# A hybrid recurrent decoder layer on one core: output projection in one pair of PSUM banks, layer norm transposes after the next block's gates and GLU, one Newton root for two tiles, gates ahead of GLU

## The chip, the cores and the metric

The kernel runs on one core of a Trainium2 chip. The metric is the device time of one execution in microseconds (us). The engines are called as in the profile: PE (matrix engine), PEld (its weight loads), DVE (vector), ACT (activation), POOL (GpSimd), SP (sync, which issues DMAs).

## What is computed

One decoder layer over 2048 prompt rows and 32 sample rows of width 1024, all in float32:

```python
z = h @ in_proj                                   # [gate | xa | xb], 512 columns each
xa_c = causal_dwconv(xa)                          # width 4
r, gi = sigmoid(xa_c @ w_r + b_r), sigmoid(xa_c @ w_i + b_i)
a = exp(-8 * r * softplus(-lam))
hseq = linear_scan(a, sqrt(1 - a * a) * gi * xa_c)
y_a = gelu(gate) * hseq
gy = gelu(s5_ssm(xb))
y_b = gy * sigmoid(gy @ glu_w + glu_b)            # the GLU
mix = concat([y_a, y_b]) @ out_proj
x = layer_norm(ALPHA * x + g1 * mix)
f = square(relu(h2 @ mlp_w1 + b1)) @ mlp_w2       # h2: x, scaled and shifted
x = layer_norm(ALPHA * x + g2 * f)
```

Float32 products are made of three matmuls on split operands (high x high, low x high, high x low), so that each operand is split beforehand into a high part (a copy on ACT) and a low part (a subtraction on DVE or POOL).

## The kernel before, in words

The program has four stages: modulation, input projection and the S5 scan (to about 440 us of the trace), then the stage that the change touches (about 440 to 765 us), then the MLP in three groups of rows (to the end). The stage in the middle goes over the prompt in eight blocks `pi` of 256 rows, each with these pieces:

- `rg_gates` (L301): eight gate products of 3 matmuls, 256 columns wide, each into a bank of its own; ACT takes each out with a Sigmoid, then makes four Tanh tiles `th` from the results. 24 matmuls a block.
- `glu_block` (L896): loads `gy` (four DMAs on SP, L850), splits it, makes four GLU tiles of 12 matmuls (48 a block), a Tanh in place on the bank (ACT, L913), and takes each out with `stt` into `gy` on DVE (L914); then splits the product into `ybh` and `ybl`.
- `out_block` (L930): two tiles of 128 rows, each with two halves of 512 columns. One half is 24 matmuls of 512 columns into one bank (L962 to L964); DVE multiplies the bank by the gate row (L965) and adds the row of x, scaled (L966), after which the bank is free. So four such outputs and 96 matmuls a block. The x rows come by one DMA a tile on SP (L935) into `raw`, a pool of three buffers.
- `norm` (L976), after each tile: statistics of the two halves (L981), their aggregate, the inverse root of the variance by an integer first guess and three Newton rounds on 128x1 columns (`rstd_of`, L626: ten DVE instructions a tile), the scaled row (L984), eight PE transposes into the two banks `C` (L995), two ACT copies into `nT` (L996; one buffer, tag `res`) and one DMA to `Nd` on SP (L997). The MLP reads `Nd`.
- `rg_scan` (L321): Exp, Square, DVE product, Sqrt on ACT (the "root" in the table order), two POOL products, four DVE scans (L347), the product `gt` and its split `yah`, `yal`.
- `rg_conv` (L271): the convolution on DVE, and its split.

The loop over `pi` (L1019) writes them in the order GLU of block `pi+1`, gates of `pi+2`, output of `pi`, scan of `pi+2`, convolution of `pi+3`. This order is not the order of the queues: the framework takes it as the priority of each instruction and fixes each engine's queue when the program is built, by a model of the times. On the chip each queue is then strictly in order. `after_all` adds order alone, here between ACT functions that need different tables: GLU Tanh after the Sqrt of the block's scan, Exp after the block's Sigmoids and after an earlier GLU's Tanh.

PSUM has eight banks under four tags `A` to `D`, two each. Gates and GLU take `A` and `B` in turn, the outputs `D` and `B` in turn (L204), the transposes `C`. The MLP's first products use `A`, `D`, `B`. In the last block (`pi == 7`) the 32 sample rows come first (`oq`, L946), the first MLP weights and operands are made beside it (`first_h`, L687), and the norms of the two prompt tiles are put off into the MLP (`deferred`).

Of the kernel before, what the change touches and what calls it, by code (L numbers as in the profile page):

```python
# [13 lines left out]
ALU = mybir.AluOpType  # L14
# [21 lines left out]
def trunk(ctx: ExitStack, tc: tile.TileContext, *args):  # L36
# [167 lines left out]
    GLU_BANKS, OUT_BANKS = "AB", "DB"  # L204
# [421 lines left out]
    def rstd_of(pool, mv, nm, np_):  # L626
        r = pool.tile([P, 1], F32, tag="rstd", name=nm, bufs=2)[:np_]
        v = pool.tile([P, 1], F32, tag="rvar", name=nm + "v", bufs=2)[:np_]
        t = pool.tile([P, 1], F32, tag="rtmp", name=nm + "t", bufs=2)[:np_]
        ts(V, v, mv[:, 1:2], EPS, None, ALU.add)  # L630
        V.tensor_scalar(t.bitcast(I32), v.bitcast(I32), 1, None, ALU.arith_shift_right)
        V.tensor_scalar(r.bitcast(I32), t.bitcast(I32), -1.0, 1597463007.0, ALU.mult, ALU.add)
        ts(V, v, v, -0.5, None, ALU.mult)
        for _ in range(3):
            stt(t, r, v, r, ALU.mult, ALU.mult)
            stt(r, t, 1.5, r, ALU.add, ALU.mult)
        return r
# [258 lines left out]
    def glu_block(pi):  # L896
# [27 lines left out]
        if pi:  # L924
            after_all(rgs[pi]["root"], glu_t)
        if pi < 7:
            rgs["glu", pi + 1] = glu_t
        return yh, yl

    def out_block(pi, ya, yb):  # L930
        t0 = pi * 256
        tiles = ([(256, TS, True)] if pi == 7 else []) + [(0, P, False), (P, P, False)]
        for ti, (o, w, smp) in enumerate(tiles):
# [33 lines left out]
            work = lambda *x, at=(pi, ti, xt, w, smp, t0 + o): norm(*at, *x)  # L967
            if pi == 7 and ti in DEFER:
                deferred.append(work)
            else:  # L970
                work(p4)
# [4 lines left out]
    def norm(pi, ti, xt, w, smp, t, pool):  # L976

        st = pool.tile([P, 2, 6], F32, tag="st5", name=f"st_{pi}_{ti}", bufs=2)
        mv = pool.tile([P, 2], F32, tag="mv5", name=f"mv_{pi}_{ti}", bufs=2)
        for half in range(2):  # L980
            V.bn_stats(st[:w, half, :], xt[:w, half * 512:half * 512 + 512])  # L981
        V.bn_aggr(mv[:w], st[:w])
        rs = rstd_of(pool, mv[:w], f"rs4_{pi}_{ti}", w)
        ts(V, xt[:w], xt[:w], mv[:w, 0:1], rs, ALU.subtract, ALU.mult)  # L984
# [34 lines left out]
    for pi in range(8):  # L1019
        if pi < 7:  # L1020
            ybs[pi + 1] = glu_block(pi + 1)
        if pi < 6:
            rg_gates(rg, pi + 2)
# [15 lines left out]
        out_block(pi, rgs[pi]["ya"], ybs.pop(pi))  # L1039
# [859 lines left out]
```

## Time and profile before

| | us |
|---|---|
| median of 3 runs | 2112.32 |
| lowest, highest | 2111.28, 2117.05 |
| profiled execution, its time | 2115.44 |
| its span on the core | 2113.7 |

The profile page gives PE busy for 2011.9 us (95%), DVE 1543.5 (73%), ACT 1087.4 (51%), POOL 494.0 (23%). These are means over stages with different limits, so the stage that is changed is read by itself, from windows of the trace. In a timeline row the figures are start, duration, engine, line, operation, output and inputs; brackets give the idle time of the engine before it and what ended it.

### The profile page before, as it was taken

The page shows a single profiled execution, that of the slowest core. Times are in us where ns is not written, and L with a number is a line of the kernel's source. Part 1 is how long each engine was busy: PE and PEld are TensorE (multiplying, and loading weights), DVE is VectorE, ACT ScalarE, POOL GpSimd, SP SyncE. Part 2 cuts the span into 40 slices and gives each one's busy share as a digit, 9 for nine tenths or more (in the row PEclk, how much of TensorE's full clock was granted, in tenths as well). Part 3 has the DMA queues.
Part 4 walks back from the last instruction along what each step waited for, and adds up shares of the span by engine and source line. Part 5 has one row for each costly group of instructions (what it writes and reads, how often), then busy time and mean ns, then how long its engine had stood idle before and what let it go on. Part 6 is the DMA issues. An engine that isn't in the chain of part 4 may idle for free.

```text
span 2113.7 us, 35579 instructions
## 1 busy us (share of the span) xinstructions
PE 2011.9 (95%) x13055; PEld 1904.1 (90%) x13055; DVE 1543.5 (73%) x2920; ACT 1087.4 (51%) x2077; POOL 494.0 (23%) x327
## 2 busy tenths in 40 slices
PE   7998999889999989999999899999999999999996
PEld 4897888887877879999999899999999999999996
DVE  5678897467887899989898965666747555655587
ACT  3446665445766447554646454635445344444452
POOL 2255333323433233222223300101012001010103
PEclk9999999999999999999999999999999999999998
DMA  9799765543434467968677797878678968686861
GB/s 329 177 263 274 233 197 171 141 137 80 130 94 99 134 244 265 346 248 306 239 278 264 266 323 248 305 268 288 243 260 317 315 229 282 216 270 239 265 218 54
DMA packets 363037, 489.08 MB, mean 231 GB/s; under 512 B 126939, under 2 KB 264575, under 8 KB 362863
## 3 DMA queue, kind: packets, MB, share of 16 engines
q1 hardware_dynamic: 359415, 485.52, 69.6%
q8 instruction: 103, 1.69, 0.3%
q10 hardware_dynamic: 3448, 1.29, 0.2%
q14 instruction: 71, 0.58, 0.1%
HBM read 347.73 MB, written 139.00 MB: 230 GB/s over the span
## 4 chain that ended last, share of the span: by engine, by line
PE 63%; DVE 19%; DMA 6%; issue 5%; ACT 4%; POOL 1%; SPq 1%; ACTq 0%; DVEq 0%; POOLq 0%
PE m1a L1078 19%; PE m2x L1225 13%; PE m1s L1078 8%; PE m2s L1225 6%; PE m2a L1225 3%; DVE xc L62 2%; DVE acc L44 1%; PE accg L373 1%; PE accg L374 1%; PE accg L375 1%; PE op L963 1%; PE pa L185 1%; PE op L964 1%; PE op L962 1%; DVE gi L347 1%
## 5 line engine op out<-in xcount | busy, mean ns | idle before, releaser
L44 POOL TENSOR_TENSOR y<-y,ln_g 128x512 f32<-128x512 f32 (+3 forms) x28 | 36.5, 1320 | 645.8 <-ACT y L65 544.2
L65 ACT ACTIVATE hid<-hid 128x346 f32<-128x346 f32 (+1 forms) x240 | 116.1, 489 | 71.1 <-DVE hid L62 64.3
L65 ACT ACTIVATE ht<-hid 128x692 fp32r<-128x692 f32 (+1 forms) x92 | 72.0, 783 | 127.8 <-PE m2a L1225 38.9
L44 DVE TENSOR_TENSOR lt<-hid,ht 128x692 fp32r<-128x692 f32 (+1 forms) x92 | 85.2, 927 | 40.5 <-ACT ht L65 40.5
L44 DVE TENSOR_TENSOR acc<-m2x,acc 128x346 f32<-128x346 f32 (+1 forms) x168 | 84.1, 511 | 32.0 <-PE m2x L1225 31.7
L44 DVE TENSOR_TENSOR hid<-hid,hid 128x692 f32<-128x692 f32 (+1 forms) x92 | 87.1, 947 | 23.5 <-ACT hid L65 23.3
L1225 PE MATMUL m2x<-ht,hw2s 128*128 128x348 f32 (+1 forms) x352 | 87.7, 322 | 1.8 <-DVE acc L44 1.8
L62 DVE SCALAR_TENSOR_TENSOR hid<-m1s,vecB,u 128x346 f32<-128x346 f32 (+1 forms) x94 | 53.5, 573 | 45.0 <-ACT u L65 35.4
L65 ACT ACTIVATE u<-m1a 128x346 f32<-128x346 f32 (+1 forms) x96 | 43.5, 453 | 70.4 <-PE m1a L1078 63.0
L44 DVE TENSOR_TENSOR lb<-hid,hb 128x692 fp32r<-128x692 f32 (+1 forms) x69 | 69.2, 1004 | 4.7 <-ACT hb L65 4.5
L65 ACT ACTIVATE hb<-hid 128x692 fp32r<-128x692 f32 (+1 forms) x69 | 53.8, 783 | 21.6 <-PE m2a L1225 6.9
L1225 PEld LDWEIGHTS m2x<-ht,hw2s 128*128 128x128 f32 x352 | 61.9, 189 | 2.2 <-ACT hw2s L65 2.1
L65 ACT ACT_TABLE_LOAD x40 | 51.3, 1283 | 15.9 <-DVE hgb L57 6.5
L44 DVE TENSOR_TENSOR acc<-m2s,acc 128x346 f32<-128x346 f32 (+1 forms) x120 | 55.7, 508 | 4.1 <-PE m2s L1225 4.0
L1078 PE MATMUL m1s<-h2t13h,hw1s 128*128 128x348 f32 (+1 forms) x200 | 54.1, 329 | 3.9 <-DVE x L62 3.5
L1225 PE MATMUL m2x<-lt,hw2s 128*128 128x348 f32 (+1 forms) x176 | 56.1, 321 | 0.9 <-DVE lt L44 0.9
L1225 PE MATMUL m2x<-ht,w2s 128*128 128x346 f32 (+1 forms) x216 | 55.9, 321 | 0.0
L1225 PE MATMUL m2s<-ht,hw2s 128*128 128x348 f32 (+1 forms) x208 | 53.2, 331 | 2.6 <-ACT ht L65 2.6
L44 DVE TENSOR_TENSOR u<-m1s,u 128x346 f32<-128x346 f32 (+1 forms) x48 | 24.7, 514 | 42.0 <-PE m1s L1078 27.2
L65 ACT ACTIVATE y<-y,AB,mods 128x128 f32<-128x128 f32 (+2 forms) x96 | 37.5, 472 | 34.5 <-DMA y<-Cd 34.5
L1225 PE MATMUL m2a<-hb,hw2a 128*128 128x348 f32 (+1 forms) x200 | 52.0, 327 | 3.4 <-DVE acc L44 3.4
L1078 PE MATMUL m1a<-h2b1h,hw1a 128*128 128x348 f32 (+1 forms) x208 | 55.1, 323 | 0.0
(854 smaller groups left out, 7982.0 us busy)
## 6 DMA issues: line engine op xcount, KB each, us to landing
W1d<-hw1s SPq DMA_DIRECT2D x53, 512.0 KB
W2d<-hw2s SPq DMA_DIRECT2D x53, 512.0 KB
w1s<-W1d SPq DMA_DIRECT2D x45, 512.0 KB
lw1s<-W1d SPq DMA_DIRECT2D x43, 512.0 KB
hw2s<-W2d SPq DMA_DIRECT2D x41, 512.0 KB
hw1s<-W1d SPq DMA_DIRECT2D x40, 512.0 KB
w2s<-W2d SPq DMA_DIRECT2D x40, 512.0 KB
lw2s<-W2d SPq DMA_DIRECT2D x39, 512.0 KB
```

What stands on the lines that cost most here:

```text
L44: return eng.tensor_tensor(out=out, in0=in0, in1=in1, op=op)
L62: return V.scalar_tensor_tensor(out, in0, s, in1, op0, op1)
L65: return S.activation(out, in_, f, **kw).ins
L185: PE.matmul(pa[q:q + 32, :], cT[:, k + e, :], w[:, n * 512:n * 512 + 512], start=(k == 0), stop=(k == KD - 2), tile_position=(0, q))
L347: V.tensor_tensor_scan(gi[:, f, :n], rr[:, f, :n], gi[:, f, :n], 0.0 if pi == 0 else rgs["h"][:, f:f + 1], ALU.mult, ALU.add)
L373: PE.matmul(acc[:, :nt], wh[:, k, :], hh[:, kk, :nt], start=(k == 0), stop=False)
L374: PE.matmul(acc[:, :nt], wh[:, k, :], hl[:, kk, :nt], start=False, stop=False)
L375: PE.matmul(acc[:, :nt], wl[:, k, :], hh[:, kk, :nt], start=False, stop=(k == KD - 1))
L962: PE.matmul(ac[:w, :], yh[:, kk, o:o + w], wh[:, hs], start=(k == 0), stop=False)
L963: PE.matmul(ac[:w, :], yl[:, kk, o:o + w], wh[:, hs], start=False, stop=False)
L1078: PE.matmul(ps, x[:, k, :], h[:, k, o:o + w], start=(on is None and k + i == 0), stop=(k == 3 and i == 2), skip_group_check=on is not None)
L1225: PE.matmul(ps[2 * s_ + jj], x[:, f, js], h[:, f, :], start=(fresh and n + f + e == 0), stop=(n == len(pairs) - 1 and f + e == 3), skip_gr ...
```

## The change

The outputs rotate over the two banks `D` alone. The loop writes the gates of `pi+2` ahead of the GLU of `pi+1`. The norm is cut in two: statistics, root and scaled rows of both tiles of a block together, and the transposes, copies and stores (`norm_out`), which the next turn of the loop writes after its gates and GLU. The root is taken on a 128x2 column, so that a round of three instructions (two products, one `stt`) replaces a round of two. The GLU's Tanh is ordered after the first Sigmoid of the gates now written ahead of it, and the Exp of a scan after the GLU's Tanh of the same turn.

```diff
-    GLU_BANKS, OUT_BANKS = "AB", "DB"
+    GLU_BANKS, OUT_BANKS = "AB", "D"
...
-    def rstd_of(pool, mv, nm, np_):
-        r = pool.tile([P, 1], F32, tag="rstd", name=nm, bufs=2)[:np_]
-        v = pool.tile([P, 1], F32, tag="rvar", name=nm + "v", bufs=2)[:np_]
-        t = pool.tile([P, 1], F32, tag="rtmp", name=nm + "t", bufs=2)[:np_]
-        ts(V, v, mv[:, 1:2], EPS, None, ALU.add)
+    def rstd_of(pool, var, nm, np_):
+        r, v, t = (pool.tile([P, 2], F32, tag=tag, name=nm + tag, bufs=2)[:np_, :var.shape[1]]
+                   for tag in ("rstd", "rvar", "rtmp"))
+        ts(V, v, var, EPS, None, ALU.add)
...
         for _ in range(3):
-            stt(t, r, v, r, ALU.mult, ALU.mult)
+            mul(V, t, r, r)
+            mul(V, t, t, v)
             stt(r, t, 1.5, r, ALU.add, ALU.mult)
         return r
...
-        if pi:
+        if 0 < pi < 7:
+
+            after_all(rgs[pi + 1]["sig"][:1], glu_t)
+        elif pi:
             after_all(rgs[pi]["root"], glu_t)
         if pi < 7:
-            rgs["glu", pi + 1] = glu_t
+            rgs["glu", pi] = glu_t
...
-            work = lambda *x, at=(pi, ti, xt, w, smp, t0 + o): norm(*at, *x)
+            at = [(pi, ti, xt, w, smp, t0 + o)]
             if pi == 7 and ti in DEFER:
-                deferred.append(work)
+                deferred.append(lambda pool, at=at: norm(at, pool)())
+            elif pi == 7:
+                norm(at, p4)()
             else:
-                work(p4)
+                both_ += at
+        return norm(both_, p4) if pi < 7 else None
...
-    def norm(pi, ti, xt, w, smp, t, pool):
+    def norm(tiles, pool):
+        pi, ti = tiles[0][:2]
+        w = tiles[0][3]
+        mv = pool.tile([P, 2, 2], F32, tag="mv5", name=f"mv_{pi}_{ti}", bufs=2)
+        for e, (_, ti_, xt, *_) in enumerate(tiles):
+            st = pool.tile([P, 2, 6], F32, tag="st5", name=f"st_{pi}_{ti_}", bufs=2)
+            for half in range(2):
+                V.bn_stats(st[:w, half, :], xt[:w, half * 512:half * 512 + 512])
+            V.bn_aggr(mv[:w, e, :], st[:w])
+        rs = rstd_of(pool, mv[:w, 0:len(tiles), 1], f"rs4_{pi}_{ti}", w)
+        for e, (_, _, xt, *_) in enumerate(tiles):
+            ts(V, xt[:w], xt[:w], mv[:w, e, 0:1], rs[:, e:e + 1], ALU.subtract, ALU.mult)
+        return lambda: [norm_out(*x, pool) for x in tiles]
+
+    def norm_out(pi, ti, xt, w, smp, t, pool):
...
     for pi in range(8):
+        if pi < 6:
+            rg_gates(rg, pi + 2)
         if pi < 7:
             ybs[pi + 1] = glu_block(pi + 1)
-        if pi < 6:
-            rg_gates(rg, pi + 2)
+        if pi:
+            rows_out()
...
-        out_block(pi, rgs[pi]["ya"], ybs.pop(pi))
+        rows_out = out_block(pi, rgs[pi]["ya"], ybs.pop(pi))
```

## Rows read from the trace of the kernel before

**Rows 1.** The chain that ended last, 516.4 to 665 us, its shares by line.
```profile
by line: DVE xc L62 13.6%; DVE gi L347 8.5%; issue 8.4%; DVE rs_0t L62 7.3%; DVE ybl L44 6.2%; DVE st L981 5.4%; DVE x L62 4.5%; DMA gt<-Gd 4.4%; DVE th L62 3.4%; DMA x<-in_x_prompt_dram 3.4%; DVE op L44 3.1%; DVE gy L62 3.1%; DVE xc L59 3.
```

**Rows 2.** Busy time by stretch: five blocks, the end of the loop, two slow stretches.
```profile
core 0: us, PE busy (x) PEld busy (x) DVE busy (x) ACT busy (x) POOL busy (x), PEclk, DMA share, GB/s
516.40:692.40 176.00, 163.16 (x880) 138.00 (x879) 144.28 (x327) 119.50 (x179) 64.81 (x31) 0.98 0.38 100
692.40:732.40 40.00, 40.00 (x210) 33.90 (x209) 33.10 (x90) 14.64 (x23) 8.31 (x6) 1.00 0.39 123
560.00:570.00 10.00, 10.00 (x50) 8.76 (x50) 9.86 (x28) 7.83 (x15) 0.55 (x1) 0.87 0.54 138
670.00:680.00 10.00, 10.00 (x52) 8.61 (x52) 6.06 (x14) 7.84 (x15) 0.29 (x1) 0.91 0.82 182
```

**Rows 3.** PE's waits, 516.4 to 692.4 us: total, times, longest.
```profile
PE pg L311 <- DVE gy L62: 4.4, 7, 1.2
PE glu L910 <- DVE x L62: 3.9, 3, 1.7
PE nt L995 <- DVE x L59: 3.6, 4, 2.4
PE nt L995 <- ACT ybh L65: 0.7, 1, 0.7
```

**Rows 4.** DVE's groups by line, 516.4 to 692.4 us.
```profile
L62 DVE SCALAR_TENSOR_TENSOR rs_0t<-rs,rs_0v 128x1 f32<-128x1 f32 x17 | 12.6, 740 | 0.2
L62 DVE SCALAR_TENSOR_TENSOR rs<-rs_0t,rs 128x1 f32<-128x1 f32 x16 | 3.9, 241 | 0.1
L62 DVE SCALAR_TENSOR_TENSOR rs_1t<-rs,rs_1v 128x1 f32<-128x1 f32 x15 | 3.7, 245 | 0.2
L62 DVE SCALAR_TENSOR_TENSOR rs<-rs_1t,rs 128x1 f32<-128x1 f32 x15 | 2.3, 155 | 0.2
...
L57 DVE TENSOR_SCALAR rs_0v<-mv 128x1 f32<-128x1 f32 x5 | 0.8, 154 | 0.2
```

**Rows 5.** One output of 24 matmuls: PE's matmuls on `op`, by stretch.
```profile
609.30:614.87 5.57, 5.57 (x25) 4.31 (x23) 0.00 (x0) 1.00 0.32 124
```

**Rows 6.** Timeline of DVE, 607 to 620 us.
```profile
607.76 0.69 DVE L981 BATCH_NORM_STATS2 st<-x 128x6 f32<-128x512 f32 x1
614.80 1.23 DVE L62 SCALAR_TENSOR_TENSOR th<-xc,th 128x1024 f32<-128x1024 f32 x1 [6.35 <-ACT xc L65]
615.95 0.69 DVE L44 TENSOR_TENSOR op<-op,g1r 128x512 f32<-128x512 f32 x1
616.67 0.69 DVE L62 SCALAR_TENSOR_TENSOR x<-x,op 128x512 f32<-128x512 f32 x1
```

**Rows 7.** Timeline of PE: the end of the output that those two DVE rows take out.
```profile
609.07 0.39 PE L964 MATMUL op<-lwo,ybh 128*128 128x512 f32 x1
609.30 0.40 PE L962 MATMUL op<-hwo,yah 128*128 128x512 f32 x1
```

**Rows 8.** Timeline of DVE: root instructions and their neighbours, 656 to 667 us.
```profile
656.90 1.10 DVE L62 SCALAR_TENSOR_TENSOR rs_0t<-rs,rs_0v 128x1 f32<-128x1 f32 x1
...
663.28 0.15 DVE L62 SCALAR_TENSOR_TENSOR rs<-rs_0t,rs 128x1 f32<-128x1 f32 x1
...
664.28 2.04 DVE L62 SCALAR_TENSOR_TENSOR rs_0t<-rs,rs_0v 128x1 f32<-128x1 f32 x1
```

**Rows 9.** Timeline of POOL in the same stretch.
```profile
655.58 2.40 POOL L44 TENSOR_TENSOR gi<-gi,th 128x1024 f32<-128x1024 f32 x1 [2.73 <-ACT th L65]
663.93 2.37 POOL L44 TENSOR_TENSOR yal<-gt,yah 128x1024 fp32r<-128x1024 f32 x1 [5.94 <-ACT yah L65]
```

**Rows 10.** ACT's groups by line, 516.4 to 692.4 us.
```profile
L65 ACT ACT_TABLE_LOAD x23 | 29.5, 1283 | 0.8 <-issue 0.4
...
L65 ACT ACTIVATE nT<-nt 128x512 f32<-128x512 f32 x20 | 10.9, 589 | 1.8 <-PE nt L995 1.8
```

**Rows 11.** The chain that ended last in order of time, about 540 us: one load of 512 KB.
```profile
540.28 5.05 DMA x<-in_x_prompt_dram
```

**Rows 12.** The DMA queue's waits on SP, 500 to 765 us.
```profile
SPq L935 <- DVE x L59: 40.8, 5, 20.8
...
SPq L850 <- DVE xc L62: 17.7, 3, 9.3
```

**Rows 13.** Timeline of DVE in the last block: two outputs of its first prompt tile.
```profile
726.59 0.69 DVE L44 TENSOR_TENSOR op<-op,g1r 128x512 f32<-128x512 f32 x1
...
752.07 0.67 DVE L62 SCALAR_TENSOR_TENSOR x<-x,op 128x512 f32<-128x512 f32 x1
```

**Rows 14.** Timeline of PE in the last block: its third prompt output, and the MLP's wait.
```profile
742.37 0.50 PE L962 MATMUL op<-hwo,yah 128*128 128x512 f32 x1
...
758.27 0.66 PE L1078 MATMUL m1s<-h2t13h,hw1s 128*128 128x348 f32 x1 [3.48 <-DVE x L62]
```

More of the change, by code (lines that the diff above doesn't have):

```diff
@@ L932, in out_block @@
         tiles = ([(256, TS, True)] if pi == 7 else []) + [(0, P, False), (P, P, False)]
+        both_ = []
         for ti, (o, w, smp) in enumerate(tiles):
@@ L966, in out_block @@
                 stt(xt[:w, hs], xt[:w, hs], ALPHA, ac[:w, :])
-            work = lambda *x, at=(pi, ti, xt, w, smp, t0 + o): norm(*at, *x)
+            at = [(pi, ti, xt, w, smp, t0 + o)]
             if pi == 7 and ti in DEFER:
-                deferred.append(work)
-            else:
-                work(p4)
+                deferred.append(lambda pool, at=at: norm(at, pool)())
+            elif pi == 7:
+                norm(at, p4)()
+            else:
+                both_ += at
+        return norm(both_, p4) if pi < 7 else None
     DEFER = (1, 2)
     deferred = []
-    def norm(pi, ti, xt, w, smp, t, pool):
[L978 to L984, printed above, removed]
+    def norm(tiles, pool):
[12 more added lines that the diff above has]
+    def norm_out(pi, ti, xt, w, smp, t, pool):
         if smp:
```

## The prediction

> **What bounds the kernel now.** I read the page first, then the windows, to find the stage that the change touches and to see whether PE is idle in it. From 516.4 to 692.4 us the loop does five like blocks, 35.2 us each, and PE is busy for 163.16 of 176.0 us: 12.84 us idle [rows 2]. In the next 40 us, where gates and scans have run out, PE is busy throughout, so only the five blocks have anything to give. The view of PE's waits shows to whom that idle time goes: 4.4 us of gate matmuls waiting for the bank that a GLU tile holds until DVE has taken it out, 3.9 us of GLU matmuls waiting for a bank that an output holds, 3.6 and 0.7 us of transposes waiting for the scaled rows of the norm and for ACT [rows 3]. Together 12.6 us, nearly all of it. The chain of waits then says why they are long: until 665 us no PE line stands among its largest shares; they are DVE's, convolution, scans, `ybl`, and 7.3% for the first root's products alone [rows 1]. DVE is at 82% (144.28 of 176 us), with a queue that mostly runs late: an output ends at 609.46 us [rows 7] while DVE stands idle for 6.35 us, until ACT's Square is done, and the output's sum with x is over only at 617.36 [rows 6], 7.9 us after its last matmul.
>
> **The change part by part.**
>
> Roots. DVE spends 12.6 + 3.9 + 3.7 + 2.3 us on the root's `stt` in the five blocks [rows 4], and on four small instructions a tile, eight groups of 0.7 to 0.9 us like the one shown, 6.3 us: 28.8 us in all, 5.8 a block. New: 13 instructions a block instead of 20. At the 0.154 to 0.155 us of the rows without a stall, and 0.17 with what lies between them, that is 2.2 us. Many of the 12.6 us are no arithmetic: the root instruction at 656.90 takes 1.10 us and the one at 664.28 takes 2.04, where the one between takes 0.15 [rows 8]; they end when the POOL operations of 655.58 and 663.93 end [rows 9]. One such meeting costs 1.9 us, so a joint root costs 2.2 to 4.1 us a block. Saved: 1.7 to 3.6 us of DVE a block, 8.4 to 18 us in five. The Trainium skill (SBUF — State Buffer, "Who interferes with whom") says that a DVE instruction with two SBUF inputs is shut out while a GpSimd instruction that reads SBUF runs. By that rule the six new products are as exposed as the old `stt`; the trace agrees (rows 8 beside rows 9). By this rule the joint root is no safer than the old ones, and where it meets POOL in every block the saving is the lower of the two figures. The second column adds nothing that I count.
>
> Banks and gates. With the outputs in `D` alone, no GLU tile waits for an output: −3.9 us. With gates written first, they find banks that the last GLU left long before, and each is set free by a Sigmoid on ACT: −4.4 us. The GLU behind them waits for Sigmoids instead: 0 to 6.4 us, the upper end if each block's first Sigmoid is late by a table load of 1.28 us [rows 10]. ACT is idle for 56.5 of 176 us [rows 2], and outputs lie ready on PE meanwhile, so I take nothing.
>
> Transposes. They move behind gates and GLU of the next turn: −3.6 − 0.7 us. With each tile go eight matmuls, two copies on ACT (0.589 us each, [rows 10]) and a store on SP. As both tiles now come together and `nT` has one buffer, the second tile's copies stand on ACT until the first tile's store has landed; no row shows a store's landing, and the nearest is a load of the same size, 5.05 us [rows 11]. Behind it on ACT wait whatever Tanh, Exp or split the queue holds. Bounds 0 to 5 us a block against 11.3 us a block of idle ACT; I take nothing, since ACT is not on the path except through the Square. The x buffers are held longer, too: the load of the block's second tile stands on SP until transposes have read a buffer, as it does now (40.8 us in five waits), with `gy` and `Nd` behind it [rows 12]. I take nothing: `gy` is wanted a GLU later.
>
> Order of ACT. There are 23 table loads in five blocks, 1283 ns each [rows 10]; with GLU's Tanh behind a Sigmoid, one load a block should go: 6.4 us of ACT, hidden, as ACT idles. On the other side an Exp now waits for the four Tanh of the same turn's GLU. This lengthens the loop Sigmoid, Tanh, Exp, Square, Sqrt, scan; priced below as a rival.
>
> So DVE, which carries the path, loses 8.4 to 18 us, and PE can take no more than its 12.84 us idle. I take **−12.6**: the middle of DVE's saving is 13.2, just over it. Clock: in two stretches of 10 us the granted clock is 0.87 and 0.91 [rows 2], 2.2 us lost, behind PE's longest waits; half comes back, **−1.1** (0 to −2.2).
>
> New waits. An output is 24 matmuls in 5.57 us [rows 5]. With two banks the third output may start only when the first is out; the second covers 5.57 us. DVE takes 1.4 us when prompt (the two rows of 0.69), and 7.9 us when late: 2.3 over the cover. A block has four outputs, so 20 in the five blocks: 0 to 46 us. I take **+3**, a little over one overrun in five blocks, nearer to the prompt end: gates, GLU and transposes also lie between the outputs, about 10 us a block (163.16 / 5 = 32.6 us busy, less 4 x 5.57), more than 4 x 2.3.
>
> The last block has five uses of the pair: sample rows and four prompt outputs. Now its first prompt output is multiplied at 726.59 but added to x only at 752.07 [rows 13], since x comes late; the third begins at 742.37 [rows 14]. With one pair the third would stand until 752.74: 0 to 10.4 us. But the MLP waits anyway until 758.27 for a bank that DVE frees, 3.48 us [rows 14], and x gets its buffer sooner when both tiles' transposes come together. I take **+2**.
>
> Sum: −12.6 − 1.1 + 3 + 2 = −8.7. The profiled execution took 2115.44 us (span 2113.7), so 2106.7; that execution is 3.1 us above the median of 2112.32, so the forecast is **2103.6** (−0.41%). About 0.3%, 6.3 us, is what a measurement of this kernel can tell from no change.
>
> **The rivals.**
>
> DVE and ACT keep the pace. PE's waits are an effect of a loop through DVE and ACT: if that loop stays at 35.2 us, PE only waits elsewhere. For: the chain has no PE in it; DVE's longest stall (6.35 us at `th`) is ACT's, which no edit shortens, and Exp gets one more wait. If each joint root meets two POOL operations, 2.2 + 3.8 = 6.0 us, DVE saves nothing at all against 5.8. The queues are also fixed by a model when the program is built, so the transposes may lie where they lay. Against: root instructions are on the chain, and 7 of 20 are gone. Time: 2112.3, give or take 5.
>
> The pair `D` is the new bound (slower). Place: PE at the first matmul of every third output. If DVE stays as late as in rows 6, each output overruns its cover by 2.3 us; if half of the 20 have no other work in between, 10 x 2.3 = 23 us. With the tail's 2 and the 13.7 won above: +11.3, so 2123.6. It decides from about six overruns on (13.7 / 2.3). For: of late evictions there are many; DVE waits for ACT in its own order. Against: that lateness is partly the root work that goes, and while PE waits DVE catches up.
>
> More is won. All bounds at their good ends: −12.84 − 2.2, nothing for the pair or the tail, is −15.0, 2097.3; should the blocks before 516 us and the MLP's start gain another 4 us from an emptier DVE, 2093.
>
> **How the numbers follow.** Forecast with its better end 0.56 (of that, better than 2097 about 0.10), pace kept 0.27, pair `D` 0.17. These are also the chances of faster, same and slower. The range reaches from 2093 to 2119: it takes in the second case, and the third up to half of its price. The forecast's own range is 2097 to 2106.
>
> **What would show it.** In the profile after: five blocks take about 33 us each instead of 35.2, PE's idle time in them is below 5 us; no wait of GLU on `x L62` and none of gates on `gy L62`; transposes without a wait; root products half as many (one group instead of `rs_0` and `rs_1`), 10 to 20 us in the five blocks; 18 to 19 table loads where there were 23; the third output of a block starting without a gap. Wrong it would be if PE waits at `op` for `x L62` for over 10 us in total, if the blocks still take 35 us with DVE waiting for ACT, or if the gain made by the last block is lost between 720 and 770 us.

## The result: slower by 1.05%, and the profile after

| | before | after |
|---|---|---|
| median (lowest to highest), 6 runs each, same chip | 2113.15 (2109.27 to 2117.05) | 2135.85 (2132.01 to 2138.12) |
| ratio to before, 95% interval | | 1.0105 [1.0090, 1.0121] |
| profiled execution, its span | 2115.44, 2113.7 | 2134.54, 2132.8 |

22.7 us are lost where 8.7 were forecast as won. To see where, I compare the two profiled executions, which differ by 19.1 us, at equal work of TensorE: the matmul records are taken in order, each counted as its columns at 2.4 GHz and 10 ns, and the table says how many us later than in before the same count is reached. (A figure is good to 1 or 2 us.)

```
time in before   504   553   626   700   715   728   738   767   785   850   985  1104  1208
after           -2.0  -1.2   5.9   6.9   7.0  29.2  24.4  23.5  21.7  21.4  21.4  21.4  18.9
```

So there are three parts: about 9 us are lost in the blocks (from −2.0 to 7.0), 15 in the last block (715 to 785 us), and 3 come back late in the MLP. The blocks first, five of them from scan to scan in each trace: 37.5 us a block (187.70 / 5) where [rows 2] had 35.2. The windows:

```profile
core 0: us, PE busy (x) PEld busy (x) DVE busy (x) ACT busy (x) POOL busy (x), PEclk, DMA share, GB/s
504.20:691.90 187.70, 169.86 (x906) 143.66 (x906) 155.76 (x290) 111.37 (x174) 63.30 (x31) 0.96 0.35 93
691.90:727.00 35.10, 33.38 (x173) 27.96 (x171) 27.70 (x58) 13.21 (x21) 9.78 (x7) 1.00 0.29 85
727.00:755.80 28.80, 13.35 (x45) 9.60 (x45) 22.01 (x44) 15.91 (x26) 9.34 (x7) 0.59 0.63 212
```

PE is idle for 17.8 us in five blocks instead of 12.8, and DVE is busier than before, not less: 31.2 us a block (155.76 / 5) against 28.9 (144.28 / 5). The third row is the hole in the last block: PE busy for 13.35 of 28.8 us, at a granted clock of 0.59. PE's waits in the five blocks of after, to be set against [rows 3]:

```profile
PE pg L311 <- ACT rr L65: 9.1, 4, 3.4
PE op L966 <- DVE x L62: 4.0, 4, 1.8
PE nt L1009 <- DVE x L59: 3.7, 1, 3.7
PE nt L1009 <- ACT nT L65: 0.7, 1, 0.7
```

The two waits for banks that the change was aimed at are gone (gates for `gy`, GLU for `x`). In their place gates wait for banks that ACT's Sigmoid holds, outputs wait for the pair `D`, and the transposes wait as long as before. DVE's groups in the same stretch, to be set against [rows 4]; then ACT's, against [rows 10]:

```profile
L347 DVE TENSOR_TENSOR_SCAN gi<-rr,hp,gi 128x256 f32<-128x256 f32 x20 | 17.8, 943 | 9.4 <-POOL gi L44 9.4
...
L57 DVE TENSOR_SCALAR rs_0rvar<-mv 128x2 f32<-128x2 f32 x5 | 5.9, 1185 | 0.2
L630 DVE TENSOR_SCALAR rs_0rtmp<-rs_0rvar 128x2 int32<-128x2 int32 x5 | 5.3, 1051 | 0.2
L44 DVE TENSOR_TENSOR rs_0rtmp<-rs_0rstd 128x2 f32<-128x2 f32 x15 | 4.6, 307 | 0.3
...
L44 DVE TENSOR_TENSOR rs_0rtmp<-rs_0rtmp,rs_0rvar 128x2 f32<-128x2 f32 x15 | 2.4, 161 | 0.5
L62 DVE SCALAR_TENSOR_TENSOR rs_0rstd<-rs_0rtmp,rs_0rstd 128x2 f32<-128x2 f32 x15 | 2.4, 160 | 0.5
```

```profile
L65 ACT ACT_TABLE_LOAD x17 | 21.8, 1283 | 5.9 <-DVE gi L347 3.9 <-DMA gt<-Gd 1.8
```

The table loads fell by six where five were forecast (17, from 23). The roots fell from 28.8 to 22.2 us only: with the two small groups not shown (0.8 each), 5.9 + 5.3 + 4.6 + 2.4 + 2.4 + 1.6. A scan step takes 943 ns on average; in before it is 732, as the section on why the prediction was wrong shows.

The last block, PE's timeline of after:

```profile
731.38 0.43 PE L1094 MATMUL m1a<-h2b1h,hw1a 128*128 128x348 f32 x1 [4.40 <-ACT hw1a L65]
...
740.27 0.66 PE L1094 MATMUL m1a<-h2b1h,hw1a 128*128 128x348 f32 x1 [6.63 <-ACT h2b1h L65]
...
743.90 2.89 PE L1009 MATMUL nt<-ident,x 128*128 128x128 f32 x12 [1.38 <-DVE x L59]
747.69 1.11 PE L1009 MATMUL nt<-ident,x 128*128 128x128 f32 x4 [0.90 <-ACT nT L65]
...
755.82 0.64 PE L950 MATMUL oq<-hwo,ysum 128*32 128x256 f32 x8
...
762.86 0.50 PE L966 MATMUL op<-hwo,yah 128*128 128x512 f32 x1
```

The transposes are those of block 6. The same stretch of before, its last transposes and its `oq`, with two of block 7's outputs ahead of them:

```profile
731.66 0.39 PE L964 MATMUL op<-lwo,ybh 128*128 128x512 f32 x1
731.89 1.03 PE L995 MATMUL nt<-ident,x 128*128 128x128 f32 x8
...
732.93 0.32 PE L1078 MATMUL m1a<-h2b1l,hw1a 128*128 128x348 f32 x1
...
735.32 0.64 PE L946 MATMUL oq<-hwo,ysum 128*32 128x256 f32 x8 [0.58 <-DVE ysum L44]
```

So the last transposes of block 6 came 16 us later (747.69 instead of 731.89), the sample rows' product `oq` 20 us later, and no prompt output of block 7 starts until `oq` is through, at 762.86, where before had two of the four behind it by 732 us and began the third at 742.37 [rows 14]. The MLP's first products, `m1a`, are all that PE can do meanwhile, one at a time as their operands appear. The chain that ended last, in order of time, says what stands between the rows of block 6 and `oq` in after:

```profile
747.66 3.09 DMA Nd<-nT
750.86 0.61 ACT nT L65
751.51 1.89 PE g1p L886 x8
753.40 2.49 PE m1a L1094 x9
755.89 7.04 PE oq L950 x128
```

The first is the store of the first tile's transposed rows, which must land before the one buffer `nT` takes the second tile's; `g1p` is the transposition of the sample rows' gate values, in the banks `C` too.

Why are the rows of block 6 late? DVE's timeline from the aggregate to the scaled rows; 12 other instructions, 7.9 us, stand there beside the 13 of the root (the expectation of run 13 says 13 and 8.7):

```profile
730.28 0.21 DVE L992 BATCH_NORM_AGGREGATE mv<-st 128x2 f32<-128x12 f32 x1
731.36 0.69 DVE L44 TENSOR_TENSOR hw1a<-rw,hw1a 128x512 fp32r<-128x512 f32 x1 [0.88 <-ACT hw1a L65]
731.97 0.16 DVE L57 TENSOR_SCALAR rs_0rvar<-mv 128x2 f32<-128x2 f32 x1
732.04 0.88 DVE L44 TENSOR_TENSOR h2t42l<-nf,h2t42h 128x696 fp32r<-128x696 f32 x1
...
733.44 0.16 DVE L630 TENSOR_SCALAR rs_0rtmp<-rs_0rvar 128x2 int32<-128x2 int32 x1
...
742.75 0.16 DVE L62 SCALAR_TENSOR_TENSOR rs_0rstd<-rs_0rtmp,rs_0rstd 128x2 f32<-128x2 f32 x1
742.95 1.54 DVE L59 TENSOR_SCALAR x<-x,mv,rs_0rstd 128x1024 f32<-128x1024 f32 x2
```

`rw`, `hw1a`, `nf`, `h2t42l` are the first MLP weights and operands, which this block prepares. From the end of the aggregate (730.49) to that of the rows (744.48) it is 14.0 us; three of the root's own instructions take 0.9 to 1.6 us in it, all beside POOL instructions, which is another 3.2 us. In before, for the block's last tile, it is 4.1 (724.13 to 728.20), with two other instructions between; the first split of an MLP weight comes behind the rows:

```profile
723.93 0.21 DVE L982 BATCH_NORM_AGGREGATE mv<-st 128x2 f32<-128x12 f32 x1
...
727.38 0.81 DVE L59 TENSOR_SCALAR x<-x,mv,rs 128x1024 f32<-128x1024 f32 x1
730.88 0.69 DVE L44 TENSOR_TENSOR hw1a<-rw,hw1a 128x512 fp32r<-128x512 f32 x1 [2.68 <-ACT hw1a L65]
```

### The profile page after: what moved, and what is told of

Same layout as the page of the kernel before. It is cut to its first block, busy times and chain, and to the rows that moved or that the text cites. A ratio compares the mean times of both kernels' runs of the same rounds, so it can differ in the third digit from the quotient of the medians.

```text
span 2132.8 us, 35539 instructions
## 1 busy us (share of the span) xinstructions
PE 2015.0 (94%) x13055; PEld 1904.3 (89%) x13055; DVE 1556.8 (73%) x2880; ACT 1080.0 (51%) x2073; POOL 496.4 (23%) x327
## 4 chain that ended last, share of the span: by engine, by line
PE 62%; DVE 18%; DMA 7%; ACT 5%; issue 4%; POOL 2%; SPq 1%; ACTq 0%; DVEq 0%; POOLq 0%
PE m1a L1094 19%; PE m2x L1241 13%; PE m1s L1094 7%; PE m2s L1241 6%; PE m2a L1241 3%; DVE xc L62 2%; PE pa L185 1%; DVE acc L44 1%; PE accg L373 1%; DVE gi L347 1%; PE accg L374 1%; PE accg L375 1%; DMA xa<-Xd 1%; DVE xc L59 1%; PE op L968 1%
## 5 line engine op out<-in xcount | busy, mean ns | idle before, releaser
L966 PE MATMUL op<-hwo,yah 128*128 128x512 f32 x128 | 51.6, 403 | 4.1 <-DVE x L62 4.0
L62 DVE SCALAR_TENSOR_TENSOR E<-E,et 128x16 f32<-128x16 f32 (+3 forms) x128 | 46.0, 398 | 10.3 <-ACT et L65 10.2
```

Source lines behind the costliest of these rows:

```text
L62: return V.scalar_tensor_tensor(out, in0, s, in1, op0, op1)
L966: PE.matmul(ac[:w, :], yh[:, kk, o:o + w], wh[:, hs], start=(k == 0), stop=False)
```

## The experiments

All times are medians of 4 to 12 executions, with the ratio to before's runs on the same chip (medians 2113.6 to 2114.5). Nothing is left out of the computation in any of them. "Late" is the lag of the trace at equal work, in us at 715 (blocks), 785 (last block) and 1104 us of before (MLP).

| run | kernel | us | ratio [95%] | late at 715, 785, 1104 |
|---|---|---|---|---|
| | after | 2135.85 | 1.0105 [1.0090, 1.0121] | 7.0, 21.7, 21.4 |
| 1 | after, block 7 on D and B | 2132.16 | 1.0083 [1.0068, 1.0098] | 7.8, 11.7, 21.7 |
| 2 | after, gates behind GLU | 2139.15 | 1.0122 [1.0105, 1.0139] | 9.4, 23.9, 23.3 |
| 3 | 1 and 2 | 2135.39 | 1.0100 [1.0086, 1.0113] | 8.2, 12.4, 20.7 |
| 4 | before, pair D | 2139.65 | 1.0121 [1.0105, 1.0137] | 14.8, 22.4, 28.3 |
| 5 | 1, block 6 tile by tile | 2130.01 | 1.0072 [1.0059, 1.0085] | 7.9, 7.4, 13.2 |
| 6 | after, D and B throughout | 2127.45 | 1.0067 [1.0055, 1.0080] | 2.1, 4.9, 12.6 |
| 7 | before, joint root, late transposes | 2125.80 | 1.0057 [1.0044, 1.0069] | 0.7, 4.0, 13.7 |
| 8 | before, joint root | 2122.43 | 1.0045 [1.0031, 1.0059] | −3.1, 1.4, 2.0 |
| 9 | before, gates ahead | 2133.80 | 1.0093 [1.0078, 1.0108] | 14.7, 13.4, 14.8 |
| 10 | before, pair D in blocks 0 to 6 | 2131.48 | 1.0088 [1.0070, 1.0105] | 14.8, 14.6, 18.0 |
| 11 | 7, block 6 tile by tile | 2122.93 | 1.0039 [1.0026, 1.0053] | 3.0, 3.6, 3.2 |
| 12 | 8, block 6 tile by tile | 2115.52 | 1.0006 [0.9996, 1.0017] | −1.0, −4.1, −2.9 |
| 13 | after, MLP held | 2130.18 | 1.0078 [1.0062, 1.0094] | 5.5, 13.4, 16.6 |
| 14 | 8, MLP held | 2116.91 | 1.0019 [1.0009, 1.0029] | 0.1, 3.0, 6.0 |
| 15 | before, B and D instead of D and B | 2119.44 | 1.0024 [1.0012, 1.0036] | −1.6, 2.9, 4.9 |
| 16 | after, transposes at once | 2143.93 | 1.0141 [1.0124, 1.0157] | 9.2, 24.6, 29.0 |
| 17 | 1 and 13 | 2128.78 | 1.0067 [1.0054, 1.0080] | 7.9, 9.2, 11.5 |
| 18 | 7, MLP held | 2121.28 | 1.0034 [1.0023, 1.0044] | 3.4, 6.1, 6.5 |

A median and a trace can differ by some us: in runs 8, 9, 11 and 17 the profiled execution took 4 to 8 us less than the median (2114.87, 2129.41, 2117.01, 2124.34), in run 14 it took 4 more (2121.16). What the others lost or won there is not seen.

### Runs 1 to 4: the last block's banks, the gates, the pair

The first theory was that the jump in the last block is the four outputs queued behind `oq` in one pair (T), and the blocks' loss is the gates ahead of the GLU (G). Run 1:

```diff
-                aq = rot(OUT_BANKS, f"oq{pi}")
+                aq = rot("DB", f"oq{pi}")
...
-                    ac = rot(OUT_BANKS, f"op{pi}_{ti}_{half}")
+                    ac = rot(OUT_BANKS if pi < 7 else "DB", f"op{pi}_{ti}_{half}")
```

> Kernel after, but the joint product oq and the four outputs of block 7 rotate over banks D and B again, as before; blocks 0 to 6 stay in pair D. Theory T (the jump of about 18 us between 715 and 760 us arises because the four outputs of block 7 stand behind oq in the one pair of banks, and oq waits for the rows of block 6): about 2118 to 2121 us, the first prompt outputs of block 7 start ahead of oq again, near 725 to 735 us. Rival N (the jump comes from the late root and the late transposes of block 6, whatever the banks): 2131 to 2136 us, with TensorE still idle at 730 to 750 us.

Run 2, and run 3 with both edits:

```diff
-        if pi < 6:
-            rg_gates(rg, pi + 2)
         if pi < 7:
             ybs[pi + 1] = glu_block(pi + 1)
+        if pi < 6:
+            rg_gates(rg, pi + 2)
...
-        if 0 < pi < 7:
-
-            after_all(rgs[pi + 1]["sig"][:1], glu_t)
-        elif pi:
+        if pi:
             after_all(rgs[pi]["root"], glu_t)
         if pi < 7:
-            rgs["glu", pi] = glu_t
+            rgs["glu", pi + 1] = glu_t
```

> Kernel after, but the gates stand behind the next block's GLU again and the table order is the old one (GLU Tanh behind the root of the block before it); pair D, the joint root and the late transposes stay. Theory G (with the gates ahead, the GLU of the next block waits behind Sigmoids that wait for the scan's buffers, about 7 us over the blocks): 2127 to 2131 us, scans about 35 to 36 us apart instead of 37.5, no wait of a gate's matmul for ACT rr above 1 us. Rival (the 7 us are the pair of banks D itself or the late transposes): 2133 to 2137 us with scans still 37 us apart. The jump behind 715 us stays in either case.

> Both edits: outputs and oq of block 7 over banks D and B, and the gates behind the GLU. Left of the change are pair D in blocks 0 to 6, the joint root and the late transposes. Theories T and G together: 2135.9 - 17 - 6 = about 2113, 2109 to 2117 us, as before the change or a little faster. If only T holds: about 2119. If only G holds: about 2130. If the two losses are one and the same (each edit alone gives all of it): 2116 to 2121, no better than the better one alone.

Run 4, the kernel before with one edit:

```diff
-    GLU_BANKS, OUT_BANKS = "AB", "DB"
+    GLU_BANKS, OUT_BANKS = "AB", "D"
```

> Kernel before with one edit: all outputs and oq in pair D, nothing else of the change. Theory T (the pair makes the last block's outputs wait behind oq): 2122 to 2131 us, TensorE idle near 735 to 755 us that the kernel before has not. Rival P (the pair stalls each third output in every block): a like sum, 2119 to 2130, but spread over the blocks, about 1 us per block and a half, with no jump behind 715 us. Rival N (pair alone harmless, the late transposes are needed for the jump): 2111 to 2116 us.

Measured: 2132.16, 2139.15, 2135.39, 2139.65. Neither theory gives the time. In run 1 the outputs of block 7 do start ahead of `oq` again and PE is busy throughout up to 740 us, but `oq` itself still starts at 756.0, since block 6's rows are as late as in after (done at 747.3, there at 744.5); of the 10 us that the trace gains by 785 us, all are lost again by 1104. Between 930 and 1130 us PE's `m2x` waits for DVE's sums for 5.0 us (2 times, longest 2.9) where in after it is 1.7 (2 times, longest 1.2), which is 3.3 of the 10; the rest of that loss is not traced.

Run 2 is 3.3 us slower than after, so beside the pair the gates ahead are not the loss that theory G held; whether they are a gain is not shown, as the control (run 15) moves by more. DVE's busy time between 500 and 700 us falls from 166.34 us in after to 148.03 in run 2: 18 us less on DVE win nothing. Run 4 shows what the pair does to a kernel in which the transposes come at once. PE's waits there, 516 to 700 us:

```profile
PE nt L995 <- DVE x L59: 13.0, 4, 4.6
```

As I read it, with four banks two more outputs were there to be run while DVE took the root; with two, the transposes stand with nothing ahead of them.

### Runs 5 to 8: the joint root and the transposes

Run 5 adds to run 1:

```diff
-            elif pi == 7:
+            elif pi >= 6:
                 norm(at, p4)()
...
-        return norm(both_, p4) if pi < 7 else None
+        return norm(both_, p4) if pi < 6 else None
...
-        if pi:
+        if 0 < pi < 7:
             rows_out()
```

> The kernel of the first run (outputs and oq of block 7 over D and B) with one more edit: the two tiles of block 6 are normalised each with a root of its own and transposed at once, as before the change. Theory N (in the last block the joint root stands on VectorE among the residual MLP's work, 15.8 us from the last eviction to x where before took 9.2, and oq starts 25 us behind that eviction instead of 12.5): 2132 - 8 to 13 = 2119 to 2124 us, oq near 742 us. Rival (the last block waits for something else, the weights' load or first_h's splits): 2130 to 2134 us.

Run 6 is after with `OUT_BANKS = "DB"`; run 7 that and the edit of run 2; run 8 is run 7 with

```diff
-        if pi:
-            rows_out()
...
         rows_out = out_block(pi, rgs[pi]["ya"], ybs.pop(pi))
+        if pi < 7:
+            rows_out()
```

> Kernel after with one edit: outputs and oq rotate over D and B in all blocks, as before; gates ahead, joint root and late transposes stay. Theory P (pair D costs each block, since both halves of the pair stay taken until VectorE's eviction; the fourth run lost about 12 us in the blocks by this edit alone): the 7 us of the blocks vanish, the last block still loses by the late root: 2118 to 2125 us. Theory G (the gates ahead cost the blocks their 7 us, the pair nothing): about as the first run, 2129 to 2134 us. If the pair is the whole loss: 2109 to 2116 us.

> Kernel before with the joint root and the late transposes alone (D and B, gates behind). Theory N: the blocks as before or some us faster, the last block 8 to 13 us later: 2117 to 2126 us. If joint root and late transposes cost nothing and only the pair does: 2109 to 2115 us.

> Kernel before with the joint root alone: both tiles of a block share one root, and the transposes stand right behind it. If the late transposes are what costs in the last block: 2109 to 2116 us. If the joint root itself does (the first tile's rows wait for the second tile's outputs): within 3 us of the run before it in this list, 2116 to 2126 us, and TensorE waits at the transposes in every block.

Measured: 2130.01, 2127.45, 2125.80, 2122.43. Run 5's `oq` starts at 749.7, not 742, and its median gains 2 us: the rows of block 6 are drawn out there, too, 13.9 us with 13 other instructions between, so the joint root as such is not what makes them late. Run 6 shows the pair at 8.4 us within the change (2135.85 − 2127.45, between the two expectations), 5 of them in the blocks (2.1 late at 715 instead of 7.0). Run 7 loses nothing in the blocks and its 11 us all later (13.6 late at 738 us), with a root of 16.1 us in block 6. But it also wins nothing in the blocks, though its DVE is busy for 149.8 us between 500 and 700 us where before's is for 158.9: here DVE is relieved as the prediction wanted. PE's waits of run 7 in that stretch tell why:

```profile
PE glu L910 <- DVE x L62: 10.8, 5, 3.9
PE pg L311 <- DVE gy L62: 2.6, 5, 1.1
```

The transposes no longer wait (3.6 us in [rows 3]); the GLU, which now runs in their place, waits for its bank instead, 10.8 us against 3.9. With the transposes at once (run 8) it is 7.2 us, and the blocks are 3 to 4 us faster than before's, for 11.2 us less of DVE (147.65). Run 8's trace loses these again in the last block and ends even with before; its median lies 8 us above that, 3.4 below run 7's, so neither the joint root nor the late transposes is cleared by it.

### Runs 9 to 12: each alone

Run 9 is before with the two hunks of run 2 reversed, so that of the change only the gates and the table order are in; run 10 is run 4 with block 7 as in run 1; runs 11 and 12 are 7 and 8 with block 6 normalised and transposed as in run 5.

> Kernel before with the gates of the second next block ahead of the next block's GLU (and the table order of the change); D and B, a root for each tile, transposes at once. From the difference of the sixth run to the seventh (1.7 us, the same edit where B is in use): 2114.4 + 1 to 3 = 2115 to 2118 us. Theory G in its first form (the loop of Sigmoid, GLU Tanh, Exp and scan lengthens every block, about 7 us): 2119 to 2123 us, with the waits of the gates' matmuls for ACT rr that the changed kernel showed.

> Kernel before with pair D in blocks 0 to 6 alone; oq and the outputs of block 7 stay on D and B. Splits the 25 us of the fourth run. If the trace of that run tells it rightly (about 12 us lost by 700 us, at transposes that stand right behind their tile's output since no further output fits the pair, and the rest in the last block): 2123 to 2129 us. If the last block alone costs the 25: 2113 to 2117 us. If the blocks cost all and the jump only moves: 2133 to 2140 us.

> The seventh run (before with joint root and late transposes) with block 6 normalised tile by tile and transposed at once. Its trace lost nothing up to 715 us, 13 us at 739 us, 7 us at 767 us and 11 us at the end. Theory N (all of it hangs on block 6): 2125.8 - 8 to 12 = 2114 to 2118 us, oq near 735 us. Rival (first_h, the weights or VectorE's order in the last block, whatever block 6 does): 2122 to 2126 us.

> The eighth run (before with the joint root, transposes at once) with block 6 tile by tile: of the change only the joint root of blocks 0 to 5 is left. Its trace stood 3 to 4 us ahead of before up to 728 us and lost it behind that. If block 6 is what lost it: 2108 to 2114 us, the fastest of all. If the gain is taken again later in any case, by VectorE's adds in the residual MLP: 2114 to 2123 us.

Measured: 2133.80, 2131.48, 2122.93, 2115.52. The gates ahead cost 20 us alone, more than either expectation, and 1.7 us where joint root and late transposes are in (run 6 against 7). PE's waits of run 9, 480 to 700 us:

```profile
PE pg L311 <- DVE x L62: 11.0, 3, 6.2
PE nt L998 <- DVE x L59: 3.7, 2, 2.2
```

Here the gates, which use `A` and `B` too, wait for the bank that an output holds. So the parts seem to depend on each other: by their waits, gates ahead want the outputs out of `B`, and the pair wants the transposes late. Alone they cost 25.2 us (run 4), 20.0 (run 9) and 11.4 (joint root and late transposes, run 7), 56.6 in all; together 22.7. In run 10 the pair loses 14.8 us in the blocks and nothing more in the last one, 17.7 at the end, so run 4's other 7 to 8 are the last block's. In run 11 `oq` came at 744.8 and not near 735, and the rows took 11.3 us again; 2.9 us is all that the edit gave to the median. Run 12, with the joint root of blocks 0 to 5 alone, is the best of all versions and no faster than before (1.0006).

### Runs 13 to 18: what draws out the root, and what an order is worth

In most traces so far late rows of block 6 had gone with the loss. Run 13 is after with one order on DVE: `first_h` and the first weights' splits come behind those rows.

```diff
-            ts(V, xt[:w], xt[:w], mv[:w, e, 0:1], rs[:, e:e + 1], ALU.subtract, ALU.mult)
+            scaled[0] = V.tensor_scalar(xt[:w], xt[:w], mv[:w, e, 0:1], rs[:, e:e + 1], ALU.subtract, ALU.mult).ins
...
-            wts = weights(0, 0)
+            with tc.issue_after(scaled[0]):
+                wts = weights(0, 0)
...
-            first_h(stage[0])
+            with tc.issue_after(scaled[0]):
+                first_h(stage[0])
```

> Kernel after, all of the change kept; the only edit is an order on VectorE: the splits of the first MLP weights and first_h stand behind the scaled rows of block 6. Theory R (block 6's joint root is drawn out because 13 of those instructions, 8.7 us, were placed between its 13 dependent steps: 14.0 us from aggregate to rows where before took 4.1): root in 4 to 6 us, oq 8 to 10 us earlier (about 747 us instead of 755.8), 2135.9 - 5 to 10 = 2126 to 2131 us. Rival (the work is the same and comes behind, so the MLP's start waits for the splits instead): 2132 to 2138 us.

Run 14 is run 8 with the same order; run 15, a control, is before with `"BD"` for `"DB"`; run 16 is after with the edit of run 8.

> The eighth run (before with the joint root, transposes at once; D and B; gates behind) with the same order on VectorE. Its root took 4.4 us already, so theory R gives little: 2116 to 2122 us, oq still 19 us behind the last eviction unless other work of the MLP stands ahead of it. If the order moves oq to 13 us as in before: 2109 to 2114 us.

> A control: before with the outputs' rotation started on the other pair (B, D instead of D, B). No instruction more or less, no bank more or less. If the queues that are built are sturdy, 2111 to 2117 us. If any edit that shifts the slots costs what the single edits cost (18 to 25 us in the fourth, ninth and tenth run), 2125 us or more: then these prices are of the built order, and none belongs to the edit as such.

> Kernel after with the transposes right behind their rows, as before the change; pair D, gates ahead and the joint root stay. If the late transposes do in the blocks what they are for (in the fourth, ninth and tenth run, where they come at once beside D or the gates, TensorE waits 11 to 13 us at transposes and gates for rows and banks): blocks lose 12 to 15 us instead of 7, the last block some 5 to 8 us less than in after: 2133 to 2142 us. If they cost and give nothing: 2125 to 2132 us.

Measured: 2130.18, 2116.91, 2119.44, 2143.93. In run 13 DVE's timeline is this, from the aggregate to the rows:

```profile
727.80 0.21 DVE L993 BATCH_NORM_AGGREGATE mv<-st 128x2 f32<-128x12 f32 x1
728.04 0.17 DVE L57 TENSOR_SCALAR rs_0rvar<-mv 128x2 f32<-128x2 f32 x1
...
730.42 1.54 DVE L996 TENSOR_SCALAR x<-x,mv,rs_0rstd 128x1024 f32<-128x1024 f32 x2
731.87 0.68 DVE L44 TENSOR_TENSOR hw1a<-rw,hw1a 128x512 fp32r<-128x512 f32 x1
```

3.95 us where it was 14.0, and `oq` starts at 742.1 instead of 755.8. The median gains 5.7 us; the lag at 785 us is 13.4 instead of 21.7, and 3 us of it are lost again in the MLP. So the trace bears out theory R: the root is late because work of the MLP was placed between its dependent steps. (The 5.7 us alone would not show it: the control below moves by as much.) It is a matter of when that work becomes ready: in before the rows were done at 728.2 and the first `hw1a` came at 730.88; the aggregate of after, 6 us later, finds that work ready and has DVE to share. The same happens to before's own root, on one column: in runs 4, 9, 10 and 15, where block 6's last aggregate ends 5 to 17 us later than in before, it takes 7.4, 10.4, 6.6 and 9.2 us to the rows, with 6 to 10 other instructions between. Run 14, where the root had not been late, gains 5.5 us on run 8's median all the same, while its trace is 6 us longer than run 8's and its `oq` starts 20.6 us behind the last eviction as against 19.0; what that is, these runs don't show.

The control is 5.8 us slower (1.0024), between the two expectations, without an instruction more or less: by so much the built order alone can move this kernel. The 20 and 25 us of runs 4 and 9 are beyond that, but a difference of 3 us between two versions, as for the gates in run 2, need not belong to the edit.

Run 16 shows that the late transposes are worth 8 us beside the pair and the gates, but not where it was expected: by its lags 2 of them are in the blocks, 1 in the last block and 5 in the MLP. Outputs there wait for the pair for 7.9 us between 480 and 700 us, where after has 4.0.

The last two put the parts together.

> Kernel after with both edits of the last block: oq and the outputs of block 7 over D and B (first run, 3.7 us), and the MLP's splits held behind block 6's rows (thirteenth run, 5.7 us and 10 us of the trace at 850 us). If banks and late root are the two causes of the jump: nothing lost between 715 and 785 us, the blocks' 7 us stay and the residual MLP takes 3 to 6 us again: 2120 to 2126 us. If one of the two covers the other: 2127 to 2131 us, as the thirteenth run.

> The seventh run (before with joint root and late transposes, D and B, gates behind: 2125.8 us, 16.1 us from aggregate to rows in block 6, 13 us lost at 739 us) with the MLP's splits held behind block 6's rows. Theory R: root in 4 to 6 us, 2114 to 2119 us. Rival (the late transposes themselves lose the last block, however early the rows are): 2122 to 2127 us.

Measured: 2128.78 and 2121.28. In run 17's trace the last block loses 1.3 us (7.9 at 715, 9.2 at 785) where after loses 14.7: the pair behind `oq` and the late rows of block 6 are the whole jump, as far as that trace goes, and it is one that took 4.4 us less than the median. The median gains 7.1 us, which lies in the range of the rival, that one of the two covers the other. Run 18 brings 4.5 of the 7 to 12 us that theory R gave it: its rows take 5.3 us and not 16.1, but `oq` still starts 17.8 us behind the last eviction, where before took 12.5, and its median lies between the two expectations; that the transposes stand behind PE's other work there, as the rival has it, is not tested by itself.

## Why the prediction was wrong, step by step

- **"So DVE, which carries the path, loses 8.4 to 18 us ... I take −12.6"** is the step that fails for the blocks: it turned time saved on DVE into time saved by PE. Run 7 has the joint root and the late transposes without pair and gates; its DVE is busy for 9.1 us less than before's between 500 and 700 us, and at 715 us it is 0.7 late. Run 8 has 11.2 us less and is 3.1 early. Run 2 has 18 us less than after and gains nothing. PE's waits move to another bank instead (GLU for `x`, 10.8 us in run 7). This is the rival "DVE and ACT keep the pace". In after itself it doesn't even come to that, for DVE was not relieved.
- **"Saved: 1.7 to 3.6 us of DVE a block."** 6.6 us in five blocks, 1.3 a block, below the range; a joint root takes 4.4 us (22.2 / 5) where 2.2 to 4.1 were forecast. The sum allowed one meeting with POOL a block at most. In the five blocks of after seven root instructions are held up, for 12.8 us in all; in before there were ten, for 13.1 us, in twice as many roots. The saving is that of the fewer instructions, and the time lost to POOL hardly shrank. Six of the seven are TENSOR_SCALARs on two columns, which the prediction held to be free ("the second column adds nothing that I count"). One such meeting in after, DVE's row and then POOL's, and an instruction of the same kind on one column in before, beside the POOL instruction of 655.58 [rows 9]:

```profile
512.84 2.42 DVE L630 TENSOR_SCALAR rs_0rtmp<-rs_0rvar 128x2 int32<-128x2 int32 x1
```

```profile
512.83 2.40 POOL L44 TENSOR_TENSOR yal<-gt,yah 128x1024 fp32r<-128x1024 f32 x1 [5.05 <-ACT yah L65]
```

```profile
656.27 0.16 DVE L57 TENSOR_SCALAR rs_0v<-mv 128x1 f32<-128x1 f32 x1
```

  In the traces of all versions together, 142 of the root's TENSOR_SCALARs on 128x1 ran beside a POOL instruction, and none took over 0.16 us; of 84 on 128x2, 68 took over 0.3 us, up to 2.42. The Trainium skill (VectorE: DVE Perf Modes, "Mode 2×_2P") says that an instruction with a single source, from SBUF to SBUF, whose outermost non-unit dimension is even (or odd and equal for source and destination) may be run over both read ports. The Trainium skill (SBUF — State Buffer, "Who interferes with whom") says that an instruction in such a mode contends with GpSimd, and that one of the two then fully blocks. The traces agree for two columns; that one column goes free is told by the traces alone.

  What a root on one column would have cost here is not tested; the products behind it are held up by POOL too (one of the seven is a product, 2.34 us). And with the same two columns run 2, in which only the gates stand behind the GLU again, has its roots at 12.9 us, 2.6 a block, inside the forecast. So what brings DVE's work beside POOL's is the order of the gates. The scan steps show it as well, here for 500 to 700 us in before and in run 9 (before with gates ahead); in after and in run 2 (after with gates behind) the means are 943 and 734 ns:

```profile
L347 DVE TENSOR_TENSOR_SCAN gi<-rr,hp,gi 128x256 f32<-128x256 f32 x20 | 13.5, 732 | 0.5 <-POOL gi L44 0.5
```

```profile
L347 DVE TENSOR_TENSOR_SCAN gi<-rr,hp,gi 128x256 f32<-128x256 f32 x20 | 23.4, 1223 | 15.2 <-POOL gi L44 15.2
```

  In all versions with the gates ahead the mean is 0.91 us or more (two to five of the 20 steps take over 1 us, beside POOL); in those with the gates behind it is 0.73 to 0.74, but for the pair on before (runs 4 and 10), where it is 0.84 with one such step. The prediction priced the gates ahead by PE's banks only.
- **"−3.9", "−4.4", "−3.6 − 0.7": the waits removed.** They went as said, apart from the transposes (3.7 and 0.7 again), but others came: 9.1 us of gates waiting for ACT's Sigmoid, 4.0 for the pair. "The GLU behind them waits for Sigmoids instead: 0 to 6.4 us; I take nothing" had the right cause and the wrong place; it is the gates themselves, since eight of them in a row go through banks that only ACT sets free. "Outputs lie ready on PE meanwhile" failed: in the pair they wait as well. A block takes 37.5 us, slower than the 35.2 that the rival "DVE and ACT keep the pace" was to keep.
- **"+3" for the pair.** The waits at `op` are 4.0 us, so the sign and size of the view were right; what the pair costs the kernel is 8.4 us (run 6). The rest may be work that has to stand elsewhere in the queues since a third output does not fit; that is not shown.
- **"+2" for the last block** is the step that decides, by size: 14.7 us (the lag from 7.0 to 21.7). I bounded it by the outputs of the pair among themselves (0 to 10.4), with `oq` ahead of them at its old time. Two things were missed. Banks of one tag are given in the order of the program, where `oq` comes first, so all four outputs moved behind it; and `oq` moved back by 20 us, behind the transposes of block 6 and the rows they need; the chain goes from the rows over the transposes, the store of the one `nT` buffer (3.09 us, which I had counted as nothing) and the gate rows' `g1p` to `oq`. "x gets its buffer sooner when both tiles' transposes come together" was the reverse of what happened: the load of block 7's first prompt tile is issued at 763.00 us instead of 742.83. The joint root starts where DVE's work for the MLP begins, and I had priced it by its instructions alone.
- **Clock, −1.1.** Lost instead: 0.96 in the five blocks and 0.59 from 727 to 755.8 us, where 13.35 us of PE's busy time would be 7.9 at full clock (an estimate, 13.35 x 0.59); the low clock lies inside that hole, with 1.00 before and behind it.
- **The rival "pair D"** had the sign, with 2123.6, but not the place: outputs waited for the pair for 4 us in all, and no step of it foresaw the four behind `oq`. The text's last condition, that a gain be lost between 720 and 770 us, is where most of the loss lies.

What stays open: of the 22.7 us, 7.1 go with the two edits of run 17, and 8.4 with the pair throughout (run 6); the last block's banks are in both, so the two can't be added. Run 7, without pair and gates, still loses 11.4, of which run 18 removes 4.5. What the other 7 are is not shown, nor how much of any price under 6 us belongs to the order that the build happened to give. The late rows of block 6 (5.7 in run 13, 4.5 in run 18) are of that size: the traces show them, the times alone would not.

## What to carry to other kernels

Time taken off a busy engine need not be time won: 9 to 18 us less on DVE were worth 3 us at most here, as the waits moved to another bank. In queues that are fixed when the program is built, a chain of short dependent instructions is an invitation to put other work between them: look at what becomes ready in that stretch, and tie the chain with an order where something waits for its end. Before giving a set of banks to one use, follow every user of that tag in the program's order, the odd one in the last turn first. And parts that free each other's resources can't be priced one by one: here three parts cost 57 us alone and 23 together, and an order without any change of work already moves 6.

## What the runs showed of the hardware that was not expected

A TENSOR_SCALAR on two columns is held up by a POOL instruction where the same on one column is not (68 of 84 over 0.3 us against 0 of 142). And in the hole of the last block the clock was down for 24 us: PE is busy up to 727 us, then idle for 4.40 us; from 731.7 us, just behind the next matmul, the granted clock is 0.50, the lower of the two levels, through another 6.63 us without a matmul and the scattered work behind it, and it is 1.00 again from 755.6 us, at `oq`:

```profile
720.00:727.00 7.00, 6.98 (x31) 5.29 (x29) 4.27 (x6) 3.95 (x7) 2.25 (x3) 1.00 0.30 91
729.00:731.00 2.00, 0.00 (x0) 0.00 (x0) 1.45 (x4) 0.30 (x1) 0.00 (x0) 1.00 1.08 382
732.00:733.00 1.00, 0.96 (x4) 0.89 (x4) 1.00 (x4) 0.01 (x1) 0.00 (x0) 0.50 0.43 165
756.00:760.00 4.00, 4.00 (x80) 2.39 (x76) 1.39 (x1) 0.35 (x1) 1.03 (x1) 1.00 0.02 4
```

A 128x348 matmul behind another one is recorded with 0.32 us in before (732.93), at full clock, and with 0.49 in after at 742.03.
